# Evacuating the w_up banks by one ScalarE copy, and spreading the first Strassen group over four blocks of the MLP

## The chip, the cores and the metric

The kernel runs on one core of a Trainium2 chip. The metric is the time of one execution on the device, in microseconds.

## The reference

Two layers are computed on 256 tokens of width 1024. Each layer has a pooling mixer, a gated convolution and differential attention, whose branches are gated and merged, then the MLP and a gated embedding. The change touches the MLP alone:

```python
m = rms_norm(h, norm_mlp_g[i])
h = h + jnp.square(jax.nn.relu(m @ w_up[i])) @ w_down[i]
```

`w_up` is 1024 x 4096 and `w_down` 4096 x 1024, all in float32.

## The kernel before

Every weight comes from HBM in units of 128 x 1024 numbers. A unit is split by `WeightStream.prefetch` into a high part `whi` (ACT casts it to float32r, L243) and a low part `wlo` (DVE subtracts, L244). PE then multiplies high by high, high by low and low by high. Splits stand four units ahead of the product that uses them (`AHEAD = 4`), in five pairs of buffers, so a cast for a unit waits until PE has used the buffer's last unit. Transfers of two units each go out on SP's queue into three stage buffers.

The MLP is cut into eight blocks j of 512 hidden columns. A block has four *ups* (m = 0 to 3: 128 hidden columns by 256 tokens, `unit_c`, L414 and L416, one weight unit each) and two *downs* (f = 0, 1; `unit_a`, L376, two weight units each). An up fills a PSUM bank of the pool `bp` (four banks) with two halves of 256 columns, which have to be added, put through ReLU and squared, and split into a high and a low part: `relu_sq_c` (L959 to L965). The first block's ups take another path (`first_up`, `relu_sq`).

For blocks 0, 1 and for blocks 4, 5 (`GROUPS`), the down projection is not done by `unit_a` but by a Strassen scheme of seven products (`("S", j, n)`, `unit_s`, L385 to L389, two weight units each). Products 1, 5, 6 and 7 use `bp` banks: product 5 a bank of its own ("five"), products 1, 6 and 7 share one bank ("chain") that stays taken from product 1 to product 7. Products 2, 3 and 4 add to the downs' `acc` banks. Products 3, 5, 6 and 7 need operands that DVE and ACT make out of the squares of both blocks (`operands`, four steps behind the last up of the second block). Their weights are sums of quarters of `w_down`, made in two buffers of the pool `t8`: one DVE addition (L225) and three accumulating DMAs from POOL's queue (L216).

`mlp_order` lists ups, downs and products; the weights are packed, loaded, split and used in that order. Below it the Tile scheduler orders the instructions of each engine; each engine runs its own list in order. The work outside the MLP has the same order on every engine before and after.

Of the kernel before, what the change touches and what calls it, by code (L numbers as in the profile page):

```python
# [8 lines left out]
F32 = mybir.dt.float32  # L9
F32R = mybir.dt.float32r  # L10
AF = mybir.ActivationFunctionType
ALU = mybir.AluOpType
# [3 lines left out]
S = 256  # L16
# [18 lines left out]
GROUPS = (0, 4)  # L35


def mlp_order():

    order = []  # L40
    for j in range(0, 8, 4):
        order += [("up", b, m) for b in (j, j + 1) for m in range(4)]
        ups = [[("up", b, m), ("up", b, m + 1)] for b in (j + 2, j + 3) for m in (0, 2)]
        downs = [[("down", b, f)] for b in (j + 2, j + 3) for f in range(2)]
        prods = [[("S", j, n) for n in ns] for ns in ((1,), (5,), (3,), (6,), (7, 2), (4,))]
        for n, step in enumerate(ups + downs):
            order += step
            order += prods[n] if n < len(prods) else []
    return order


# [14 lines left out]
def weight_plan():  # L66

    plan = []
    for i in range(DEPTH):
        def a(name, ks, c):
            plan.extend(("A", name, i, k, c) for k in ks)

        def b(name, ks, cs):
            plan.extend(("B", name, i, k, c) for c in cs for k in ks)

        full, half, low, high = (0, 2, 4, 6), (0, 2), (0, 2), (4, 6)
        for ks in (low, high):
            a("w_in", ks, Q)
            a("w_in", ks, K)
        b("w_in", (0, 4), (A_IN, A_IN + 256))
        a("w_in", full, V)
        plan.append(("P", "", i, 0, 0))  # L90
        for c in (C_X, C_C, C_B):
            b("w_in", (0, 4), (c, c + 256))
        for f in range(2):
            a("w_in", full, GATE + f * 512)
        for f in range(2):
            a("w_pool_out", half, f * 512)
        for br, nm in ((1, "w_conv_out"), (2, "w_attn_out")):
            for f in range(2):
                a("w_in", full, GATE + br * D + f * 512)
                a(nm, half, f * 512)  # L100
        for ks in (low, high):
            for f in range(2):
                a("w_o", ks, f * 512)
        a("w_ple_proj", (0,), 0)
        for k in (0, 4):
            b("w_up", (k,), (0, 256))
        for what, j, n in mlp_order():
            if what == "up" and j:
                plan.append(("C", "w_up", i, 0, j * 512 + n * P))
            elif what == "down":  # L110
                a("w_down", (4 * j, 4 * j + 2), n * 512)
            elif what == "S":
                plan.extend(("S", n, i, k, j) for k in (0, 2))
        a("w_ple_proj", (0,), 512)
        for f in range(2):
            a("w_ple_gate", full, f * 512)
    return plan


def quarter(i, j, h, f):  # L120

    return tuple(("A", "w_down", i, 4 * (j + h) + k, 512 * f) for k in (0, 2))


def transfer_plan():


    out = []
    plan = weight_plan()
    u = 0  # L130
    while u < len(plan):
        if plan[u][0] != "S":
            n = 2 if u + 1 < len(plan) and plan[u + 1][0] != "S" else 1
            out.append((tuple(range(u, u + n)), tuple(plan[u:u + n])))
        else:
            n = 2
            _, prod, i, _, j = plan[u]
            at = {1: (0, 0), 3: (1, 1), 2: (1, 0)}.get(prod)
            out.append(((u, u + 1), at and quarter(i, j, *at)))
        u += n  # L140
    return out


def weight_blocks():

    place = {}
    for _, block in transfer_plan():
        if block:
            place.setdefault(block, len(place))
    for i in range(DEPTH):  # L150
        for j in GROUPS:
            place.setdefault(quarter(i, j, 0, 1), len(place))
    return place


class WeightStream:
# [10 lines left out]
    def __init__(self, ctx, tc, w):  # L167
        self.nc = tc.nc
        self.w = w
        self.plan = weight_plan()  # L170
        self.transfers = transfer_plan()
        self.place = weight_blocks()
        self.last_unit = {units[-1]: n for n, (units, _) in enumerate(self.transfers)}
        self.stage_pool = ctx.enter_context(tc.tile_pool(name="wstage", bufs=self.STAGE_BUFS))
        self.part_pool = ctx.enter_context(tc.tile_pool(name="wpart", bufs=self.AHEAD + 1))
        self.keep_pool = ctx.enter_context(tc.tile_pool(name="wkeep", bufs=1))
        self.new_sums = None
        self.sums = {}
        self.stage = {}
        self.parts = {}  # L180
        self.next_dma = 0
        self.next_split = 0
        self.pos = 0

    def load(self, parts=1, between=None):


        while self.next_dma < len(self.transfers):
            units, block = self.transfers[self.next_dma]
            self.next_dma += 1  # L190
            kind, prod, i, _, j = self.plan[units[0]]
            size = len(units) * UNIT
            if kind == "S" and prod == 1:
                if i not in self.sums:
                    self.sums[i] = self.new_sums()
                t, second = self.sums[i]
            elif block:
                t = self.stage_pool.tile([P, 2 * UNIT], F32, tag="stage", name="stage")
            else:
                t = self.sums[i][prod == 7]  # L200
            for n, u in enumerate(units):
                self.stage[u] = t[:, n * UNIT:(n + 1) * UNIT]
            if not block:
                continue
            src = self.w[self.place[block]]
            n = size // parts
            for c in range(0, size, n):
                self.nc.sync.dma_start(out=t[:, c:c + n], in_=src[:, c:c + n])
                if between is not None and c == n:
                    between()  # L210
            if kind == "S" and prod == 1:
                self.nc.sync.dma_start(out=second, in_=self.w[self.place[quarter(i, j, 0, 1)]])
            return
# [4 lines left out]
    def sums_after(self, u):  # L218

        kind, prod, i, k, j = self.plan[u]  # L220
        if kind != "S" or k != 2:
            return
        fst, snd = self.sums[i]
        if prod == 1:
            self.nc.vector.tensor_add(out=fst, in0=fst, in1=snd)  # L225
            self.add_to(snd, i, j, 1, 1)
        elif prod == 5:
            self.add_to(fst, i, j, 1, 1)
        elif prod == 6:
            self.add_to(fst, i, j, 1, 0)  # L230

    def prefetch(self, upto, between=None):
        while self.next_split < min(len(self.plan), upto):
# [28 lines left out]
def kernel(  # L262
# [10 lines left out]
    nc = tc.nc  # L273
# [28 lines left out]
    def t4v(dt=F32):  # L302
        return t4(dt)[:, 0:4 * S].rearrange("p (g t) -> p g t", t=S)

    def t2(dt=F32):
        return u2.tile([P, 512], dt, tag="t2", name="t2")
# [150 lines left out]
    def split(hi, lo, src):  # L457
        nc.scalar.copy(out=hi, in_=src)  # L458
        nc.vector.tensor_sub(out=lo, in0=src, in1=hi.bitcast(F32))  # L459
# [16 lines left out]
    for i in range(DEPTH):  # L476
        units = []
# [458 lines left out]
        def square(j, ms):  # L936

            if j - j % 2 not in GROUPS:
                return t2()[:, 0:S * (ms.stop - ms.start)].rearrange("p (m t) -> p m t", t=S)
            if ms.start == 0:  # L940
                st["f", j] = t4v()
            return st["f", j][:, ms, :]
# [13 lines left out]
        def relu_sq_c(j, m):  # L956
            if m == 0:
                st["s", j] = (t4v(F32R), t4v(F32R))
            sh, sl = st["s", j]  # L959
            bank = tiles.pop(("bp", "up", j, m))  # L960
            z, s2 = t2()[:, 0:S], square(j, slice(m, m + 1))[:, 0, :]
            nc.scalar.copy(out=z, in_=bank[:, 1, :])
            nc.vector.tensor_add(out=z, in0=bank[:, 0, :], in1=z)  # L963
            nc.vector.scalar_tensor_tensor(out=s2, in0=z, scalar=0.0, in1=z, op0=ALU.max, op1=ALU.mult)  # L964
            split(sh[:, m, :], sl[:, m, :], s2)  # L965

        def first_up(m, k):
            xs = st["x"][k // 4].rearrange("p (k a) t -> p k a t", a=2)
# [245 lines left out]
```

## Time and profile before

| | us |
|---|---|
| three runs | 872.79, 873.38, 873.44 |
| median | 873.38 |
| profiled execution, its own time | 872.22 |
| its span, first to last instruction | 870.5 |
| PE busy | 846.5 (97%) |
| DVE busy | 651.5 (75%) |
| ACT busy | 491.9 (57%) |
| a weight sum's transfer on SP's queue, issue to landing, median of 8 | 5.9 |
| one on POOL's queue, median of 12 | 8.8 |

PE is the engine that sets the end: it is busy nearly always, and its few idle stretches lie almost all in the MLP. A busy PE is read with care, since matmuls are pipelined and their ends are modelled; how far apart they start says more. The granted clock was 0.996 of full speed on the mean.

### The profile page before, as it was taken

To read this page: it belongs to the slowest core of one execution; us is meant where nothing else is said; L and a number is where in the kernel's file an instruction comes from. 1 tells how busy PE (TensorE), PEld (TensorE's weight loads), DVE (VectorE), ACT (ScalarE), POOL (GpSimd) and SP (SyncE) were. 2 spreads that over 40 slices of the span, in tenths; PEclk is the share of its full clock that TensorE was granted. 3 is DMA by queue.
4 is the path that set the end of the run, shared out by engine and by line. 5 is a ranking of instruction groups with operands and counts; after the bars stand their busy time and mean duration, and the time that the engine had idled before them with its cause. 6 is when DMAs were issued, how large, how long until landed. Compare 5 with 4: busy or idle time off the path is not lost.

```text
span 870.5 us, 11751 instructions
## 1 busy us (share of the span) xinstructions
PE 846.5 (97%) x4516; PEld 727.9 (84%) x4516; DVE 651.5 (75%) x980; ACT 491.9 (57%) x735; POOL 41.2 (5%) x46
## 2 busy tenths in 40 slices
PE   8999999999997999899999999999999899998997
PEld 6999988888986888788889998888889778887886
DVE  5987886556698858987668887855667978598874
ACT  6655464454666545665654746544456565456562
POOL 2400000000000000000023000000000000000000
PEclk9999999999999999999999999999999999999999
DMA  9755435555657774865445544555556767557541
GB/s 319 280 194 177 163 130 209 194 193 192 244 170 225 248 251 145 236 213 204 174 166 192 194 145 145 182 206 193 194 175 248 209 196 267 216 170 206 180 165 48
DMA packets 25975, 171.02 MB, mean 196 GB/s; under 512 B 3008, under 2 KB 3776, under 8 KB 5952
## 3 DMA queue, kind: packets, MB, share of 16 engines
q1 hardware_dynamic: 24048, 157.66, 49.8%
q0 software_dynamic: 1728, 12.58, 7.6%
q8 instruction: 35, 0.57, 0.3%
q14 instruction: 20, 0.16, 0.1%
q10 hardware_dynamic: 144, 0.05, 0.0%
HBM read 169.23 MB, written 1.05 MB: 196 GB/s over the span
## 4 chain that ended last, share of the span: by engine, by line
PE 92%; DVE 4%; ACT 2%; issue 1%; DMA 1%; SPq 0%; ACTq 0%
PE acc L376 49%; PE bp L414 11%; PE bp L416 5%; PE bp L403 4%; PE bp L405 4%; PE bp L401 4%; DVE wlo L244 2%; PE bp L385 2%; PE bp L387 1%; PE bp L389 1%; PE tr L437 1%; ACT whi L243 1%; PE acc L1128 1%; PE acc L387 1%; PE acc L389 1%
## 5 line engine op out<-in xcount | busy, mean ns | idle before, releaser
L244 DVE TENSOR_TENSOR wlo<-stage,whi 128x1024 fp32r<-128x1024 f32 (+1 forms) x280 | 339.1, 1214 | 168.4 <-ACT whi L243 166.6
L243 ACT CAST whi<-stage 128x1024 fp32r<-128x1024 f32 (+1 forms) x280 | 291.5, 1045 | 273.2 <-PE acc L376 147.7
L376 PE MATMUL acc<-whi,t 128*128 128x512 f32 x1248 | 396.7, 393 | 0.9 <-ACT whi L243 0.6
L376 PEld LDWEIGHTS acc<-whi,t 128*128 128x128 f32 x1248 | 233.7, 188 | 49.4 <-ACT whi L243 1.6
L376 PE MATMUL acc<-wlo,t 128*128 128x512 f32 x624 | 243.6, 390 | 0.5 <-DVE wlo L244 0.5
L376 PEld LDWEIGHTS acc<-wlo,t 128*128 128x128 f32 x624 | 117.2, 188 | 24.9 <-DVE wlo L244 1.6
L414 PE MATMUL bp<-t,whi 128*128 128x512 f32 x448 | 122.4, 395 | 5.4 <-DVE t L963 5.4
L414 PEld LDWEIGHTS bp<-t,whi 128*128 128x128 f32 x448 | 77.3, 189 | 17.7 <-issue 6.6
L401 PE MATMUL bp<-t,whi 128*128 128x256 f32 x320 | 90.5, 284 | 0.0
L403 PE MATMUL bp<-t,whi 128*128 128x256 f32 x320 | 90.5, 283 | 0.0
L405 PE MATMUL bp<-t,wlo 128*128 128x256 f32 x320 | 90.5, 283 | 0.0
L416 PEld LDWEIGHTS bp<-t,wlo 128*128 128x128 f32 x448 | 68.5, 189 | 9.3
L416 PE MATMUL bp<-t,wlo 128*128 128x256 f32 x448 | 71.2, 281 | 0.0
L403 PEld LDWEIGHTS bp<-t,whi 128*128 128x128 f32 x320 | 61.1, 191 | 0.5
L401 PEld LDWEIGHTS bp<-t,whi 128*128 128x128 f32 x320 | 61.0, 191 | 0.5
L405 PEld LDWEIGHTS bp<-t,wlo 128*128 128x128 f32 x320 | 61.1, 191 | 0.1
L244 DVE TENSOR_TENSOR wlo<-t,whi 128x1024 fp32r<-128x1024 f32 x40 | 48.9, 1222 | 11.0 <-ACT whi L243 11.0
L243 ACT CAST whi<-t 128x1024 fp32r<-128x1024 f32 x40 | 42.1, 1051 | 25.8 <-PE bp L414 15.9
L458 ACT CAST t<-t 128x256 fp32r<-128x256 f32 (+1 forms) x80 | 37.4, 469 | 24.5 <-DVE t L964 22.8
L459 DVE TENSOR_TENSOR t<-t,t 128x256 fp32r<-128x256 f32 (+1 forms) x80 | 39.6, 497 | 3.1 <-ACT t L458 2.8
L385 PE MATMUL bp<-whi,t 128*128 128x512 f32 x64 | 26.9, 420 | 11.8 <-DVE t L963 9.6
L427 ACT ACTIVATE t<-tr,par 128x256 fp32r<-128x256 f32 (+1 forms) x56 | 26.2, 502 | 20.9 <-PE tr L568 8.4
(153 smaller groups left out, 778.3 us busy)
## 6 DMA issues: line engine op xcount, KB each, us to landing
stage<-in_w_dram SPq DMA_DIRECT2D x136, 1024.0 KB, 4.8
t<-in_w_dram POOLq DMA_DIRECT2D x12, 1024.0 KB, 8.8
t<-in_w_dram SPq DMA_DIRECT2D x8, 1024.0 KB, 5.9
stage<-in_w_dram SPq DMA_DIRECT2D x4, 512.0 KB, 6.6
stage<-in_w_dram SPq DMA_DIRECT2D x4, 256.0 KB, 5.3
h<-in_x_dram SPq DMA_DIRECT2D x4, 256.0 KB, 10.0
t<-in_xT_dram SPq DMA_DIRECT2D x1, 512.0 KB, 10.1
out_dram<-h SPq DMA_DIRECT2D x2, 256.0 KB, 2.0
```

What stands on the lines that cost most here:

```text
L243: self.nc.scalar.copy(out=hi[:, cs], in_=src[:, cs])
L244: self.nc.vector.tensor_sub(out=lo[:, cs], in0=src[:, cs], in1=hi[:, cs].bitcast(F32))
L376: nc.tensor.matmul(accs[t], lhsT=lhs[:, kx + j, tk], rhs=rhs[:, j, :], start=begins[t] and j == 0 and n == 0, stop=last and j == 1 and n == 2,
L385: nc.tensor.matmul(bank, lhsT=xh[:, k + n, :], rhs=wh[:, n, :], start=first, stop=False, skip_group_check=True)
L401: nc.tensor.matmul(bp[:, m, :], lhsT=wh[:, j, ms], rhs=xh[:, kx + j, :], start=first, stop=False, skip_group_check=True)
L403: nc.tensor.matmul(bp[:, m, :], lhsT=wh[:, j, ms], rhs=xl[:, kx + j, :], start=False, stop=False, skip_group_check=True)
L405: nc.tensor.matmul(bp[:, m, :], lhsT=wl[:, j, ms], rhs=xh[:, kx + j, :], start=False, stop=last, skip_group_check=True)
L414: nc.tensor.matmul(bank, lhsT=wh[:, k, :], rhs=xk[k], start=k == 0, stop=False, skip_group_check=True)
L416: nc.tensor.matmul(bank[:, 1, :], lhsT=wl[:, k, :], rhs=xk[k][:, 0, :], start=False, stop=k == KD - 1, skip_group_check=True)
L427: nc.scalar.activation(out=hi, in_=src, func=AF.Copy, scale=g)
L458: nc.scalar.copy(out=hi, in_=src)
L459: nc.vector.tensor_sub(out=lo, in0=src, in1=hi.bitcast(F32))
```

## The change

Two things change. First, `relu_sq_c`: ACT copies the whole bank (512 columns) into SBUF, DVE adds the two halves there, ACT does the ReLU and squares twice (once into the float32r high part, once into float32), and DVE subtracts for the low part. Before, ACT copied one half, DVE added it to the other half in PSUM, DVE did ReLU and square in one instruction, ACT cast and DVE subtracted. Second, `mlp_order`: the seven products of blocks 0 and 1 no longer stand among the ups and downs of blocks 2 and 3 alone, but are spread up to the ups of block 5. The products of blocks 4 and 5 stand where they stood, up to the downs' end. As the two weight sum buffers are now in use for longer, `load` holds back the first transfer of the second group until product 4 of the first has been split.

```diff
 def mlp_order():
...
+    order = up(0, 0) + up(0, 1) + up(1, 0) + up(1, 1)
+    order += up(2, 0) + prod(0, 1) + up(2, 1) + up(3, 0) + prod(0, 5) + down(2, 0) + up(3, 1) + prod(0, 3)
+    order += down(2, 1) + prod(0, 6) + down(3, 0) + up(4, 0) + prod(0, 7) + down(3, 1) + prod(0, 2)
+    order += up(4, 1) + up(5, 0) + prod(0, 4) + up(5, 1)
+    order += up(6, 0) + prod(4, 1) + up(6, 1) + prod(4, 5) + up(7, 0) + prod(4, 3) + up(7, 1) + prod(4, 6)
+    order += down(6, 0) + prod(4, 7, 2) + down(6, 1) + prod(4, 4) + down(7, 0) + down(7, 1)
     return order
...
+            kind, prod, i, _, j = self.plan[units[0]]
+            if kind == "S" and prod == 1:
+                if self.sums_busy:
+                    self.late += 1
+                    return
+                self.sums_busy = True
             self.next_dma += 1
-            kind, prod, i, _, j = self.plan[units[0]]
...
+        elif prod == 4:
+            self.sums_busy = False
+            late, self.late = self.late, 0
+            for _ in range(late):
+                self.load()
...
-            z, s2 = t2()[:, 0:S], square(j, slice(m, m + 1))[:, 0, :]
-            nc.scalar.copy(out=z, in_=bank[:, 1, :])
-            nc.vector.tensor_add(out=z, in0=bank[:, 0, :], in1=z)
-            nc.vector.scalar_tensor_tensor(out=s2, in0=z, scalar=0.0, in1=z, op0=ALU.max, op1=ALU.mult)
-            split(sh[:, m, :], sl[:, m, :], s2)
+            both = t2().rearrange("p (a t) -> p a t", t=S)
+            nc.scalar.copy(out=both, in_=bank)
+            r = both[:, 0, :]
+            nc.vector.tensor_add(out=r, in0=r, in1=both[:, 1, :])
+            nc.scalar.activation(out=r, in_=r, func=AF.Relu)
+            s2 = both[:, 1, :] if j - j % 2 not in GROUPS else square(j, slice(m, m + 1))[:, 0, :]
+            nc.scalar.activation(out=sh[:, m, :], in_=r, func=AF.Square)
+            nc.scalar.activation(out=s2, in_=r, func=AF.Square)
+            nc.vector.tensor_sub(out=sl[:, m, :], in0=s2, in1=sh[:, m, :].bitcast(F32))
```

The PE list in the first layer, before, behind product 1 of the first group: the second up of that stretch (bank 2573, block 2, m = 3), then product 5 (bank 2603).

```order
L414 MATMUL bp_2573<-t8_2093,whi_2475 128x512 x4
L416 MATMUL bp_2573<-t8_2093,wlo_2476 128x256 x4
L414 MATMUL bp_2573<-t8_2154,whi_2475 128x512 x4
L416 MATMUL bp_2573<-t8_2154,wlo_2476 128x256 x4
L385 MATMUL bp_2603<-whi_2511,t2_2461 128x512
L387 MATMUL bp_2603<-wlo_2512,t2_2461 128x512
L389 MATMUL bp_2603<-whi_2511,t2_2462 128x512
```

The same place after (all line numbers are 18 higher): the same up is bank 2578, then come an up of block 3 (bank 2607) and the first half of down 0 of block 2 (banks acc_2692 and acc_2693).

```order
L432 MATMUL bp_2578<-t8_2093,whi_2479 128x512 x4
L434 MATMUL bp_2578<-t8_2093,wlo_2480 128x256 x4
L432 MATMUL bp_2578<-t8_2154,whi_2479 128x512 x4
L434 MATMUL bp_2578<-t8_2154,wlo_2480 128x256 x4
L432 MATMUL bp_2607<-t8_2093,whi_2515 128x512 x4
L434 MATMUL bp_2607<-t8_2093,wlo_2516 128x256 x4
L432 MATMUL bp_2607<-t8_2154,whi_2515 128x512 x4
L434 MATMUL bp_2607<-t8_2154,wlo_2516 128x256 x4
L394 MATMUL acc_2692<-whi_2608,t4_2469 128x512
L394 MATMUL acc_2693<-whi_2608,t4_2469 128x512
```

Product 5 has moved behind one up more, half a down and a further up. In the second group PE's list is the one of before, but that product 6 stands behind all four ups of block 7.

ACT's list in the second group of the first layer, before: from the cast for product 3's first unit (whi_3395) to the cast for the last up of block 7 (whi_3450). Banks 3265, 3336 and 3364 are ups of block 6 (m = 1, 2, 3); t2_3295 and t2_3358 are the squares of the ups m = 1 and m = 2.

```order
L243 CAST whi_3395<-stage_3205 128x1024
L962 COPY t2_3294<-bp_3265 128x256
L458 CAST t4_3256<-t2_3295 128x256
L458 CAST t2_3314<-t2_3312 128x512
L243 CAST whi_3405<-stage_3205 128x1024
L458 CAST t2_3331<-t2_3329 128x512
L962 COPY t2_3357<-bp_3336 128x256
L243 CAST whi_3420<-stage_3270 128x1024
L962 COPY t2_3387<-bp_3364 128x256
L458 CAST t4_3256<-t2_3358 128x256
L243 CAST whi_3450<-stage_3270 128x1024
```

The same place after: whi_3407 is product 3's first unit, whi_3462 the last up's; bank 3348 is the up m = 2 of block 6, 3376 is m = 3; bank 3406 is product 5; t2_3306 holds the up m = 1, whose bank was copied four rows ahead of this piece.

```order
L261 CAST whi_3407<-stage_3216 128x1024
L476 CAST t2_3326<-t2_3324 128x512
L983 ACTIVATE t2_3306<-t2_3306 128x256
L261 CAST whi_3417<-stage_3216 128x1024
L985 ACTIVATE t4_3268<-t2_3306 128x256
L986 ACTIVATE t2_3306<-t2_3306 128x256
L261 CAST whi_3432<-stage_3282 128x1024
L476 CAST t2_3343<-t2_3341 128x512
L261 CAST whi_3462<-stage_3282 128x1024
L980 COPY t2_3369<-bp_3348 128x512
L980 COPY t2_3399<-bp_3376 128x512
L1056 COPY t2_3429<-bp_3406 128x512
```

The copy of the up m = 1 moved ahead of product 3's cast; the copies of m = 2 and m = 3 moved behind the cast for the last up of block 7. Both layers have the same lists in their MLPs.

## Rows read from the trace of the kernel before

**Rows 1.** The page: busy time, share of the span, instructions of each engine.

```profile
PE 846.5 (97%) x4516; PEld 727.9 (84%) x4516; DVE 651.5 (75%) x980; ACT 491.9 (57%) x735; POOL 41.2 (5%) x46
```

**Rows 2.** Waits of PE: who waited for whom, us in total, times, longest us.

```profile
PE bp L385 <- DVE t L963: 9.6, 4, 2.4
PE bp L414 <- DVE t L963: 5.4, 6, 1.3
PE bp L385 <- ACT whi L243: 2.3, 2, 1.1
```

**Rows 3.** Timeline of PE, first layer: start us, us, instruction, [idle before <-releaser].

```profile
243.23 0.63 PE L416 MATMUL bp<-t,wlo 128*128 128x256 f32 x4
243.70 0.63 PE L414 MATMUL bp<-t,whi 128*128 128x512 f32 x2
...
261.97 0.47 PE L414 MATMUL bp<-t,whi 128*128 128x512 f32 x1 [1.33 <-DVE t L963]
...
267.39 0.47 PE L385 MATMUL bp<-whi,t 128*128 128x512 f32 x1 [2.39 <-DVE t L963]
...
359.03 0.47 PE L385 MATMUL bp<-whi,t 128*128 128x512 f32 x1 [2.39 <-DVE t L963]
```

**Rows 4.** Timeline of DVE and ACT ahead of the wait that ends at 359.03.

```profile
357.20 0.37 ACT L962 COPY t<-bp 128x256 f32<-128x256 f32 x1
357.32 1.23 DVE L244 TENSOR_TENSOR wlo<-stage,whi 128x1024 fp32r<-128x1024 f32 x1 [0.42 <-ACT whi L243]
358.46 0.42 DVE L963 TENSOR_TENSOR t<-bp,t 128x256 f32<-128x256 f32 x1
```

**Rows 5.** Windows: stretch, its us, busy us of each engine, PEclk, DMA share, GB/s.

```profile
318.70:346.80 28.10, 28.10 (x162) 24.55 (x161) 21.93 (x34) 15.04 (x26) 0.88 (x1) 1.00 0.48 157
346.80:378.60 31.80, 28.29 (x147) 23.86 (x146) 28.69 (x46) 21.81 (x35) 1.95 (x4) 1.00 0.85 234
695.10:699.50 4.40, 4.40 (x13) 3.46 (x13) 3.69 (x6) 2.07 (x3) 0.00 (x0) 0.61 0.50 210
267.30:271.70 4.40, 4.31 (x19) 3.63 (x20) 3.95 (x7) 3.35 (x5) 0.00 (x0) 1.00 0.55 222
```

**Rows 6.** Timeline of PE behind the wait that ends at 695.08, second layer.

```profile
695.39 0.39 PE L387 MATMUL bp<-wlo,t 128*128 128x512 f32 x1
695.62 0.39 PE L389 MATMUL bp<-whi,t 128*128 128x512 f32 x1
...
696.54 0.63 PE L389 MATMUL bp<-whi,t 128*128 128x512 f32 x1
696.97 0.63 PE L385 MATMUL bp<-whi,t 128*128 128x512 f32 x1
```

**Rows 7.** Groups by shape, ACT and DVE: xcount | busy us, mean ns | idle.

```profile
L243 ACT CAST whi<-stage 128x1024 fp32r<-128x1024 f32 x276 | 289.1, 1051 | 271.1 <-PE acc L376 147.7 <-PE bp L403 50.7 <-PE bp L414 22.9
...
L458 ACT CAST t<-t 128x256 fp32r<-128x256 f32 x56 | 22.7, 405 | 22.8 <-DVE t L964 22.8
L962 ACT COPY t<-bp 128x256 f32<-128x256 f32 x56 | 20.4, 364 | 0.0
...
L1034 ACT COPY t<-bp 128x512 f32<-128x512 f32 x4 | 2.3, 579 | 0.0
...
L540 ACT ACTIVATE t<-t 128x256 f32<-128x256 f32 x2 | 0.9, 437 | 0.0
...
L244 DVE TENSOR_TENSOR wlo<-stage,whi 128x1024 fp32r<-128x1024 f32 x276 | 336.3, 1221 | 166.3 <-ACT whi L243 164.4
...
L964 DVE SCALAR_TENSOR_TENSOR t<-t 128x256 f32<-128x256 f32 x56 | 23.5, 419 | 0.5
L963 DVE TENSOR_TENSOR t<-bp,t 128x256 f32<-128x256 f32 x56 | 23.3, 417 | 0.0
```

**Rows 8.** Timeline of ACT with a full queue.

```profile
238.42 0.63 ACT L952 ACTIVATE t<-t 128x512 fp32r<-128x512 f32 x1
238.95 0.62 ACT L953 ACTIVATE t<-t 128x512 f32<-128x512 f32 x1
```

More of the change, by code (lines that the diff above doesn't have):

```diff
@@ L38, in mlp_order, with up, down, prod @@
 def mlp_order():
[L40 to L48, printed above, removed]
+    def up(b, half):
+        return [("up", b, m) for m in (2 * half, 2 * half + 1)]
+    def down(b, f):
+        return [("down", b, f)]
+    def prod(j, *ns):
+        return [("S", j, n) for n in ns]
+    order = up(0, 0) + up(0, 1) + up(1, 0) + up(1, 1)
[4 more added lines that the diff above has]
+    order += down(6, 0) + prod(4, 7, 2) + down(6, 1) + prod(4, 4) + down(7, 0) + down(7, 1)
     return order
@@ L178, in __init__ @@
         self.sums = {}
+        self.sums_busy = False
+        self.late = 0
         self.stage = {}
@@ L230, in sums_after @@
             self.add_to(fst, i, j, 1, 0)
+        elif prod == 4:
+            self.sums_busy = False
+            late, self.late = self.late, 0
+            for _ in range(late):
+                self.load()
     def prefetch(self, upto, between=None):
```

## The prediction

> **What bounds the kernel now.** I read the page first: PE is busy 97% of the span [rows 1], and the change neither adds nor removes a matmul. So the most that any change of this kind can give is PE's lost time. The list of PE's waits says where that is: twelve waits, six in each layer, all in the MLP, 9.6 + 5.4 + 2.3 = 17.3 us [rows 2]. Ten of them end on L963, the DVE addition that is the last reader of an up's bank: PE has the weights but no free `bp` bank. The timeline shows two of the largest as a pair in the first layer's first group (1.33 and 2.39 us, ending at 261.97 and 267.39) and the largest of its second group (2.39 us, ending at 359.03) [rows 3].
>
> The idle figure is a little short. A burst of four 256-column matmuls is drawn 0.63 us long although the next burst starts 0.47 us after it [rows 3], so each wait hides 0.16 us more: 12 x 0.16 = 1.9 us, 19.2 us in all.
>
> There is a second cost. After the wait that ends at 695.08 the stretch of 4.40 us has a granted clock of 0.61 of full speed, while behind the equally long wait that ends at 267.39 it stays at 1.00 [rows 5]. At the lower level (1.2 instead of 2.4 GHz) 512-column matmuls start 0.43 us apart instead of 0.23 us [rows 6]; eight of them lose 1.6 us. The mean clock of 0.996 over 870.5 us is 3.5 us of full speed missing, of which a part lies at the very end; I take two such stretches in the second layer, 3.1 us. The removable total is 19.2 + 3.1 = 22.3 us.
>
> Why is L963 late? Ahead of 359.03, ACT's half copy of that bank ends at 357.57, but DVE is in a 1.23 us split until 358.55 and adds only then [rows 4]. In the 31.80 us of the second group's products DVE is busy 28.69 us and ACT 21.81 us [rows 5]. DVE is the full queue, and the bank waits in it.
>
> **Part 1: the bank leaves by ACT.** The bank becomes free with ACT's copy; the addition, then in SBUF, no longer holds it. Per up, ACT gives up the half copy (0.364) and the cast (0.405) and gets a 512-column copy of PSUM (0.579, L1034), a ReLU and two squares [rows 7]. A 256-column ReLU or Square from SBUF isn't in the trace. The nearest rows are the ACTIVATE of L540 (0.437) and the cast of L458 (0.405); with a full queue, instructions start about 0.1 us earlier than their length says (0.63 long, 0.53 apart) [rows 8], which gives 0.34 from below. I take 0.437 of busy time and 0.34 of pace. Busy, an up costs ACT 0.579 + 3 x 0.437 − 0.364 − 0.405 = 1.12 us more; 56 ups make 63 us, 492 to 555 us of the span. DVE loses L964 (0.419): 23.5 us less. The addition of two SBUF operands isn't shown either; its neighbours cost 0.417 and 0.419 whether they read PSUM or not [rows 7], so I leave it at 0.42.
>
> That is 63 us of new work on an engine whose time isn't on the path, so what matters is the pace where ups stand alone. There PE takes 28.10 us for ten ups (162 matmuls recorded, 16 each), 2.81 us each [rows 5]. ACT now needs, at pace, 0.95 (weight cast) + 0.48 + 3 x 0.34 = 2.45 us; with no overlap at all, 1.05 + 0.58 + 1.31 = 2.94 us. I take 2.45, as the order puts the next bank's copy or the next weight cast between an up's dependent steps. So ACT keeps pace with 0.3 us to spare, and costs nothing there; with three or four banks a lag of several us would still be hidden. If that cover were gone at 2.94, the 56 ups would lose 0.13 us each, 7 us.
>
> The Trainium skill speaks against this move: in "ScalarE: Activation LUTs", section "Rules for kernel authors", ReLU, additions and multiplications belong on VectorE and not on ScalarE. The trace has the VectorE as the fuller queue where it counts, so I don't follow it in the forecast; what it would mean is the last rival.
>
> **Part 2: the first group is spread.** I walked the new lists with these durations, with 0 at product 1 of block 0. PE does product 1 to 2.75 (twelve matmuls 0.23 us apart [rows 6]), three ups to 11.2, half a down to 13.9, an up to 16.7, and then asks for product 5's bank. That bank is the one of the second of these ups, filled at 8.4 and copied by ACT at about 14.0. The tightest point is the up in front of product 5: its bank is copied at about 13.0, PE asks at 13.9. Squares for the half down are there with about 1 us to spare too. Then downs (two weight units in 5.5 us instead of in 2.8) thin out the work for ACT and DVE, and nothing is late. So this group's four waits in each layer go, and the slow clock behind one of them.
>
> The held-back load: product 4's split stands some two ups ahead of its use, and four more ups follow it, so that it ends some 2 x 2.8 + 2.75 + 4 x 2.8 = 19.5 us before PE reaches the second group's product 1; such a transfer lands 5.9 us after its issue (the table's median). Hidden, at nothing; wholly exposed it would be 5.9 us per layer.
>
> **Part 3: the second group.** Here the products stand as before. Set 0 at its product 1. PE would do product 1 to 2.75, two ups to 8.35, product 5 to 11.1, product 3 to 13.85 and then the first up of block 7, which takes the bank of block 6's third up. The copies that free the second up's and product 5's banks, walked in the same way, end at 2.1 and 5.4 against 5.55 and 8.35, so both old waits go. But the copy for the up at 13.85 has moved behind the cast for block 7's last up. From 8.1, when PE lets go of the buffer for product 3's first cast, ACT has a full queue: cast to 9.05, operand cast to 9.6, ReLU to 9.9, cast to 10.9, two squares (the first behind the ReLU) to 11.65, cast to 12.6, operand cast to 13.1, cast to 14.05, copy to 14.6. PE waits about 0.7 us for it. That is the new wait, once in each layer: 2 x 0.7 = 1.4 us.
>
> **Sum.** 22.3 − 1.4 = 20.9 us. The profiled execution (872.22, span 870.5) becomes 851.3. The median of the runs is 1.16 us above the profiled time, so the median becomes 852.5.
>
> **Rivals.**
> - *ACT falls behind in the second group.* Without overlap, the eleven instructions of the walk take 0.1 us more each: the wait is 1.8 us instead of 0.7, 2.2 us in all, 854.7; with a slow clock after it in both layers (1.6 each) 857.9. For it: that piece of ACT's list has no gap. Against: the rows with full queues do overlap.
> - *DVE stays late.* The wait moves from the bank to what DVE still makes: the low part of the squares that the half down behind the first group's third up reads, or the low weights. If the first pair's 1.33 + 2.39 + 0.32 = 4.04 us stays in each layer, 8.1 us come back: 860.6. For it: DVE is the fuller queue. Against: it loses 0.42 us per up.
> - *Nothing is gained.* The banks are freed earlier but PE's wait was for the weight splits standing behind the same additions: 873. Against: only two of twelve waits name a weight cast.
> - *ACT sets the pace: slower.* If the five steps of an up run strictly one after the other, with ACT standing still for DVE's addition, an up costs 1.05 + 0.58 + 0.42 + 1.31 = 3.36 us against 2.81. 56 x 0.55 = 31 us are lost against 20.9 gained: 883. It decides from 2.81 + 20.9 / 56 = 3.18 us per up. For it: each ReLU waits for DVE in the middle of ACT's list. Against: other banks' copies and weight casts stand in between. This is where the skill's rule just named would lead; the trace bears it out only so far that ACT gets 63 us more.
>
> **How the numbers follow.** Forecast as summed 0.58 (its own range 850.6 to 853.9: from all 22.3 us and half a microsecond more to twice the new wait); ACT falling behind 0.22; DVE late 0.12; nothing gained 0.03; slower 0.05. The first two hold 0.80, so the range goes from 850.4 to 858.3. A difference under 0.2% (1.7 us) is not told from none by these runs. Faster 0.92, same 0.03, slower 0.05.
>
> **What would show it.** PE's waits on the addition vanish from the list of waits; in their place stands one wait per layer of 0.5 to 1 us on ACT's bank copy, at block 7's first up. The mean clock rises towards 1.00, with no slow stretch after 695 or its like. ACT is busy near 555 us, DVE near 628. Wrong would be: idle time of PE on whole weight casts in the runs of ups (ACT's pace), waits on the low parts in the first group (DVE), or a wait of 2 us and a clock of 1.2 GHz behind the copy.

## The result and the profile after

| | us |
|---|---|
| changed kernel, four runs | 850.20, 850.23, 850.36, 850.93 |
| median | 850.3 |
| kernel before, same session, median of four | 873.41 |
| ratio | 0.9732, 95% interval 0.9714 to 0.975 |
| profiled execution, its span | 850.93, 849.1 |

The kernel became 23.1 us faster. The forecast was 852.5 with a range from 850.4: the direction and the places were right, and the median lies 0.1 us below the range. On the profiled execution, against which the sum was made, 851.3 was forecast and 850.93 came out. Executed again in another session (e13 below), the changed kernel had a median of 851.4.

The page after, busy times of the engines, answers to [rows 1]. PE has 5.4 us less to show as busy although its 4516 matmuls are the same, DVE 19.2 us less, ACT 43.9 us more. PE was idle for 24.0 us of the span before, 17.3 of them in the MLP; it is idle for 8.0 us now, nearly all at the kernel's two ends.

```profile
PE 841.1 (99%) x4516; PEld 724.6 (85%) x4516; DVE 632.3 (74%) x924; ACT 535.8 (63%) x847; POOL 41.2 (5%) x46
```

All of PE's waits after, answering to [rows 2]. None of the old lines is left. The first four stand in the first 15 us, at the kernel's start; only the last, twice 0.2 us, is in the MLP.

```profile
PE acc L394 <- ACT whi L261: 1.1, 2, 0.7
PE tr L343 <- POOL ones L339: 1.0, 1, 1.0
PE acc L394 <- ACT t L445: 0.8, 1, 0.8
PE acc L394 <- DVE wlo L262: 0.5, 1, 0.5
PE acc L405 <- DVE wlo L262: 0.4, 2, 0.2
```

What is left in the second group, first layer: PE at the start of product 1, inside product 3 and at block 7's first up, then ACT's cast and copies ahead of it (start us, us, instruction, idle before).

```profile
341.06 0.40 PE L403 MATMUL bp<-whi,t 128*128 128x512 f32 x1
...
353.55 0.39 PE L403 MATMUL acc<-whi,t 128*128 128x512 f32 x1
354.11 0.50 PE L405 MATMUL acc<-wlo,t 128*128 128x512 f32 x1 [0.18 <-DVE wlo L262]
354.45 0.39 PE L407 MATMUL acc<-whi,t 128*128 128x512 f32 x1
...
355.15 0.39 PE L407 MATMUL acc<-whi,t 128*128 128x512 f32 x1
355.63 1.20 PE L432 MATMUL bp<-t,whi 128*128 128x512 f32 x4
```
```profile
354.05 1.05 ACT L261 CAST whi<-stage 128x1024 fp32r<-128x1024 f32 x1
355.00 1.06 ACT L980 COPY t<-bp 128x512 f32<-128x512 f32 x2
```

These matmuls otherwise start 0.23 us apart. From 353.55 to 354.11 it is 0.56, 0.33 too much, and 0.11 more to the next; from 355.15 to 355.63 it is 0.48, 0.25 too much, and 0.11 more behind that. So each layer keeps 0.8 us, in two pieces: one for product 3's second low part, one for the bank copy that the prediction named. Together with the waits the slow clock went. The stretch that had 0.61 is at 1.00, like the second group's (answering to [rows 5]):

```profile
695.10:699.50 4.40, 4.40 (x25) 3.78 (x24) 2.20 (x4) 2.94 (x6) 0.00 (x0) 1.00 0.72 263
346.80:378.60 31.80, 31.53 (x156) 26.07 (x156) 27.61 (x38) 26.95 (x47) 1.88 (x4) 1.00 0.77 227
```

### The profile page after: what moved, and what is told of

Its sections match the earlier page's. It is cut to its first block, busy times and chain, and to the rows that moved or that the text cites. A ratio compares the mean times of both kernels' runs of the same rounds, so it can differ in the third digit from the quotient of the medians.

```text
span 849.1 us, 11777 instructions
## 1 busy us (share of the span) xinstructions
PE 841.1 (99%) x4516; PEld 724.6 (85%) x4516; DVE 632.3 (74%) x924; ACT 535.8 (63%) x847; POOL 41.2 (5%) x46
## 4 chain that ended last, share of the span: by engine, by line
PE 96%; ACT 1%; DMA 1%; issue 0%; SPq 0%; DVE 0%
PE acc L394 50%; PE bp L432 12%; PE bp L434 6%; PE bp L423 5%; PE bp L421 5%; PE bp L419 5%; PE bp L405 2%; PE bp L407 2%; PE bp L403 2%; PE tr L455 1%; PE acc L1150 1%; PE acc L405 1%; PE acc L407 1%; PE acc L403 1%; DMA stage<-in_w_dram 1%; ACT whi L261 1%
## 5 line engine op out<-in xcount | busy, mean ns | idle before, releaser
L229 POOL DMA_DIRECT2D t<-in_w_dram x12 | 10.7, 888 | 489.5 <-ACT t L986 380.1
L446 DVE SCALAR_TENSOR_TENSOR t<-tr,par,t 128x256 fp32r<-128x256 f32 (+1 forms) x56 | 27.9, 517 | 5.3 <-ACT t L445 5.1
L980 ACT COPY t<-bp 128x512 f32<-128x512 f32 x56 | 31.6, 576 | 0.0
```

What stands on the lines that cost most here:

```text
L446: nc.vector.scalar_tensor_tensor(out=lo, in0=src, scalar=g, in1=hi.bitcast(F32), op0=ALU.mult, op1=ALU.subtract)
L980: nc.scalar.copy(out=both, in_=bank)
```

## Experiments

Line numbers in the versions with the new order are those of the changed kernel. Adding, removing or moving instructions makes the scheduler lay every list anew, so a version can differ from the changed kernel in more than its edit.

**e1: the kernel before, again.** No edit.

> The kernel before, unchanged, to see its own scatter from run to run. Theory (clock): a run's time follows the number of stretches at 1.2 GHz behind the long waits; one stretch takes 3.4 us, lowers the mean granted clock by 0.002 and costs 1.6 us, so runs with a clock of 0.996 take about 872.2 us and those with 0.994 about 873.8 us, and the median lies above the profiled 872.2 because most runs have three or four such stretches where the profile had two. Rival (start): the runs differ by the first 20 us, where PE waits for the first transfers; then the clock is the same in all runs and the times differ by under 1 us. Rival (scale): the profiled time is simply shorter than the others by about 1 us in every kernel.

Median 873.6, ratio 0.9999 (0.9987 to 1.0011). By mean granted clock, the 29 executions of this kernel in that session fall into steps: one at 0.998 (871.12), twelve at 0.996 (871.39 to 872.95), thirteen at 0.994 (873.41 to 874.40), three at 0.992 (875.28 to 875.64). The profiled one had 0.994 and three slow stretches, each around the end of one of the four longest waits (columns as in [rows 5]):

```profile
267.19:270.60 3.41, 3.23 (x8) 2.58 (x9) 2.69 (x6) 1.26 (x3) 0.00 (x0) 0.50 0.70 286
697.27:700.68 3.41, 3.41 (x10) 2.66 (x9) 2.42 (x5) 1.78 (x3) 0.00 (x0) 0.50 0.51 214
789.43:792.84 3.41, 2.97 (x7) 2.42 (x8) 2.95 (x6) 1.03 (x2) 0.00 (x0) 0.50 0.72 300
```

3.41 us at half speed lose 1.7 us, 0.002 of the span: one stretch per step. The execution shown ahead of the prediction had 0.996 and stayed at 1.00 behind 267.39, where this one falls to 0.50. Its two stretches are the one in [rows 5] and this one:

```profile
788.30:791.70 3.40, 3.37 (x8) 2.72 (x9) 2.57 (x5) 1.41 (x3) 0.00 (x0) 0.51 0.61 253
```

So its 872.22 is an execution with two stretches, and the median one has three.

**e2: the new evacuation with the old order.**

```diff
-    order = up(0, 0) + up(0, 1) + ...            # and the held-back load
+    order = []                                   # mlp_order of before
+    for j in range(0, 8, 4): ...
```

> The new evacuation in the old order. Theory (the bank waits in DVE's queue): with the bank freed by ACT both groups are like the second group of the changed kernel, where 0.8 us per layer is left; two groups in two layers leave about 3.2 of 22.3 us, some 854 us, and no stretch at 1.2 GHz. Rival (the order does it): the first group keeps its waits of 5.9 us per layer, some 862 us.

852.23, ratio 0.9757 (0.9738 to 0.9775): the theory, 1.8 us below its figure. Part 1 alone is nearly the whole gain; the first group then has the same leftover as the second, 0.8 us in each layer (the row is the counterpart of the one at 354.11), and these 1.6 us are what the spread is worth. The medians differ by 1.9 us, or by 0.8 if the changed kernel's second median is taken (e13).

```profile
267.98 0.50 PE L387 MATMUL acc<-wlo,t 128*128 128x512 f32 x1 [0.18 <-DVE wlo L244]
```

**e3: the new order with the old evacuation.**

```diff
-            both = ...; nc.scalar.copy(out=both, in_=bank); ...
+            z = t2()[:, 0:S]
+            nc.scalar.copy(out=z, in_=bank[:, 1, :])
+            nc.vector.tensor_add(out=z, in0=bank[:, 0, :], in1=z)
+            nc.vector.scalar_tensor_tensor(out=s2, in0=z, ..., op0=ALU.max, op1=ALU.mult)
+            split(sh[:, m, :], sl[:, m, :], s2)
```

> The new order with the old evacuation. Theory (the bank waits in DVE's queue): the first group's waits go since downs thin out DVE's work, the second group keeps 3.8 us per layer and its stretch at 1.2 GHz in one or both layers: some 860 us. Rival (the order does it): some 853 us. Rival (the order does nothing, the split operands are still late): some 870 us.

867.13, ratio 0.9924 (0.9908 to 0.9941): none of the three figures came. The order is worth 6.3 us, but the first group's waits did not go, even with downs between the ups. The first and the last of PE's four waits in the first layer's first group:

```profile
262.59 1.17 PE L432 MATMUL bp<-t,whi 128*128 128x512 f32 x4 [1.32 <-DVE t L981]
...
274.58 0.70 PE L432 MATMUL bp<-t,whi 128*128 128x512 f32 x2 [1.62 <-DVE t L981]
```

**e4: the bank leaves by ACT, the rest stays.** ReLU and square remain one DVE instruction, with ACT's cast behind it; new order.

```diff
             nc.scalar.copy(out=both, in_=bank)
             nc.vector.tensor_add(out=z, in0=z, in1=both[:, 1, :])
-            nc.scalar.activation(out=r, in_=r, func=AF.Relu)     # and both squares
+            nc.vector.scalar_tensor_tensor(out=s2, in0=z, ..., op0=ALU.max, op1=ALU.mult)
+            split(sh[:, m, :], sl[:, m, :], s2)
```

> The new order; ACT copies the whole bank, but ReLU and square stay one VectorE instruction and ACT casts once, as before. Theory (freeing the bank is what counts): 850 us, the same as the changed kernel within 1 us. Rival (the 0.42 us per up that VectorE is relieved of counts): the second group keeps about half its waits, some 854 us or more.

864.43, ratio 0.9891 (0.9873 to 0.991): the rival's side, but 14.1 us lost instead of some 4. "Free the bank and the wait goes" falls. ACT ahead of PE's longest wait, which ends at 272.81:

```profile
267.48 0.41 ACT L476 CAST t<-t 128x256 fp32r<-128x256 f32 x1 [1.72 <-DVE t L983]
...
268.91 1.06 ACT L261 CAST whi<-stage 128x1024 fp32r<-128x1024 f32 x1 [0.21 <-PE bp L432]
...
271.23 1.04 ACT L261 CAST whi<-stage 128x1024 fp32r<-128x1024 f32 x1 [0.49 <-PE acc L394]
272.18 1.07 ACT L980 COPY t<-bp 128x512 f32<-128x512 f32 x2
```
```profile
272.81 0.96 PE L432 MATMUL bp<-t,whi 128*128 128x512 f32 x3 [1.66 <-ACT t L980]
```

ACT has gaps of 1.72, 0.21 and 0.49 us in front of the copies: they stand behind casts that wait for DVE's squares and for PE's buffers. The bank no longer needs DVE, but its copy's place in the list does.

**e5: the other half: the bank is freed by DVE as before, ReLU and squares on ACT.**

```diff
-            nc.scalar.copy(out=both, in_=bank)
-            nc.vector.tensor_add(out=r, in0=r, in1=both[:, 1, :])
+            nc.scalar.copy(out=r, in_=bank[:, 1, :])
+            nc.vector.tensor_add(out=r, in0=bank[:, 0, :], in1=r)
```

> The changed order, and ReLU and both squares on ACT as in the changed kernel; but the bank leaves as before the change: ACT copies one half of it, and DVE's addition reads the other half from PSUM and frees it. Theory (what counts is that the DVE loses its 0.42 us instruction per up, 23.5 us in all, so that its queue is never behind; who frees the bank is of little weight): about 852, at most 1 us of leftover waits per layer more than the changed kernel. Rival (both halves of the new evacuation are needed, the bank has to leave by ACT too): the waits on the DVE's addition return, 858 to 865, near the 864.4 of the version in which only the copy was changed.

863.71, ratio 0.988 (0.9864 to 0.9897): the rival. DVE ahead of a wait of PE, then that wait: the addition that frees the bank comes behind a low part and an operand's low part.

```profile
270.22 1.23 DVE L262 TENSOR_TENSOR wlo<-stage,whi 128x1024 fp32r<-128x1024 f32 x1 [0.78 <-ACT whi L261]
271.36 0.68 DVE L477 TENSOR_TENSOR t<-t,t 128x512 fp32r<-128x512 f32 x1
271.97 0.42 DVE L981 TENSOR_TENSOR t<-bp,t 128x256 f32<-128x256 f32 x1
```
```profile
272.53 0.47 PE L432 MATMUL bp<-t,whi 128*128 128x512 f32 x1 [1.56 <-DVE t L981]
```

With the new order the four evacuations give 867.1 (old), 864.4 (copy alone), 863.7 (ReLU and squares alone), 850.3 (both): 2.7 and 3.4 us by themselves, 16.8 together.

**e6 and e14: the second group spread like the first.**

```diff
-    order += up(6, 0) + prod(4, 1) + up(6, 1) + prod(4, 5) + up(7, 0) + prod(4, 3) + up(7, 1) + prod(4, 6)
-    order += down(6, 0) + prod(4, 7, 2) + down(6, 1) + prod(4, 4) + down(7, 0) + down(7, 1)
+    order += up(6, 0) + prod(4, 1) + up(6, 1) + up(7, 0) + prod(4, 5) + down(6, 0) + up(7, 1) + prod(4, 3)
+    order += prod(4, 6) + down(6, 1) + prod(4, 7, 2) + prod(4, 4) + down(7, 0) + down(7, 1)
```

> The changed kernel, with the ups and downs of the second group put among its products as in the first one (two ups between product 1 and product 5, a half down behind product 5, product 6 right behind product 3). Theory: the two leftover spots in front of block 7's last ups, 0.8 us in each layer, go, and nothing new comes: 850.3 - 1.6 = 848.7. Rival 1: the leftovers only move to another bank or low part: 850.3. Rival 2: the products stand closer together at the end, their weight sums (8.8 us each from issue to landing) come too late, and PE waits for them: 852 to 858.

848.96, ratio 0.9713 (0.9699 to 0.9728): the theory. Its window in the second group: PE is busy throughout, and its list of waits has no line from the MLP.

```profile
346.80:378.60 31.80, 31.80 (x160) 26.91 (x159) 26.90 (x38) 26.20 (x46) 1.95 (x4) 1.00 0.82 239
```

Beside the changed kernel in one session:

> The version with the second group spread too, beside the changed kernel. Theory (the two leftover spots, 0.8 us in each layer, are gone): 1.3 to 1.6 us below the changed kernel in the same session, about 848.9. Rival (the difference of 1.3 us between the two earlier medians is one of sessions): within 0.5 us of the changed kernel.

849.29 (848.99 to 849.72) against the changed kernel's 851.4. The nine executions of this version in both sessions lie at 849.72 or below, the eight of the changed kernel at 850.13 or above. It is faster than the changed kernel by 1.3 and 2.1 us in the medians of the two sets, once under and once over what was expected. The profiled executions tell the start from the rest: with times counted from the same small matmuls on PE near 25 us, the transposes of L555 (25.37 and 25.22 here, the changed kernel's under e13), they differ by 1.57 us in the first set and by 1.56 in the second. Those are the two spots.

**e13: the changed kernel, again.** No edit.

> The changed kernel once more, unchanged, beside the kernel before in the same session. The prediction added the 1.16 us by which the kernel before's median lay above its profiled execution. Theory (that difference is slow-clock stretches behind PE's waits, whose number differs from run to run; the changed kernel has hardly any wait left): every run at a mean clock of 0.999 or 1.00 and within 1.5 us of each other, median 850.3, 0.3 us either way, at or below its profiled execution. Rival (a profiled execution is about a microsecond shorter than the median whatever the kernel): median 0.8 to 1.4 us above the profiled execution.

851.4 (851.91, 850.13, 851.32, 851.47), ratio 0.9748 (0.9733 to 0.9763), clocks 0.997 to 1.0. The rival is refuted, as the profiled execution, 851.91, is the longest. The theory is met only in part: the runs spread over 1.8 us instead of 1.5, one clock is 0.997, and the median is 0.8 us above the upper end of what was expected. For the profiled execution the profile puts all of it at the start: the MLP has the same two waits of 0.2 us as in the changed kernel's first profile, but the same transposes stand 0.97 us later, and the two times differ by 0.98 us (first profile, then this one):

```profile
25.51 0.60 PE L555 MATMUL tr<-diag,ones 128*128 128x128 f32 x4
```
```profile
26.48 0.60 PE L555 MATMUL tr<-diag,ones 128*128 128x128 f32 x4
```

PE's listed waits at the start are not longer in sum (3.1 us against 3.4), but one of them is 1.59 us long, for a weight cast that itself waited 1.89 us for its transfer, and behind it the clock falls (the last section has the row: 0.70 over 5 us, which is 1.5 us lost).

```profile
10.85 0.73 PE L394 MATMUL acc<-whi,t 128*128 128x512 f32 x2 [1.59 <-ACT whi L261]
```

Two of the other executions took 851.32 and 851.47 at a clock of 1.0; why these were longer than the first session's is open.

**e7 and e8: one and two more Squares per up on ACT.**

```diff
             nc.scalar.activation(out=s2, in_=r, func=AF.Square)
+            nc.scalar.activation(out=s2, in_=r, func=AF.Square)   # e8: twice
```

> The changed kernel with one more 256-column Square per up on ACT, 56 in all, whose result nobody needs (it writes the same values to the same place). Theory (ACT has 0.3 us to spare per up): at 0.34 us of pace each it comes to 2.79 us per up against PE's 2.81, so it costs 0 to 2 us: 850 to 852.5. Rival (ACT already sets the pace where ups stand alone): all 56 x 0.34 = 19 us show: about 869.

> The changed kernel with two more 256-column Squares per up on ACT, 112 in all. Theory (0.3 us to spare per up): the pace is 3.13 us per up against PE's 2.81, so up to 56 x 0.32 = 18 us, less where downs and products let ACT catch up: 856 to 868. Rival 1 (ACT has far more to spare than the sum said, since its share fell short of the predicted 555 us by 19 us): below 853. Rival 2 (ACT already sets the pace): 2 x 19 = 38 us: about 888.

861.96 (ratio 0.9865, 0.9844 to 0.9885) and 865.48 (0.9895, 0.9876 to 0.9914). One more costs 11.7 us, far more than forecast, the second only 3.5. e8 lies in its theory's range, but no account by pace gives both: in e8 PE never waits in the ups that stand alone, and in e7 ACT has idle time ahead of the late copy:

```profile
263.71 1.05 ACT L261 CAST whi<-stage 128x1024 fp32r<-128x1024 f32 x1 [1.76 <-PE bp L432]
...
265.50 0.56 ACT L980 COPY t<-bp 128x512 f32<-128x512 f32 x1
```
```profile
266.12 0.50 PE L432 MATMUL bp<-t,whi 128*128 128x512 f32 x1 [1.97 <-ACT t L980]
```

The copy stands behind a weight cast that waits 1.76 us for a buffer that PE still uses.

**e9 and e10: the added Squares by place.** e9 has two more in the ups of blocks 1, 4 and 5, e10 one more in those of blocks 2, 3, 6 and 7.

```diff
             nc.scalar.activation(out=s2, in_=r, func=AF.Square)
+            if j in (1, 4, 5):                                    # e10: not in, and once
+                nc.scalar.activation(out=s2, in_=r, func=AF.Square)
+                nc.scalar.activation(out=s2, in_=r, func=AF.Square)
```

> The changed kernel with two more 256-column Squares on ACT (their result is needed by nobody) in the ups of blocks 1, 4 and 5 alone, 12 ups in a layer, most of which stand outside the products. The run with one more Square in every up lost 11.6 us, at four spots per layer, all among the products. Theory A (outside the products ACT has room; the loss comes where a bank's copy stands in ACT's list behind a cast that waits): at most 1.5 us lost, 850 to 852. Theory B (ACT is simply too full: what it falls behind in the plain ups, 3.13 - 2.81 = 0.32 us in each of ten, shows as a wait at the first product after them): 2 to 3.2 us per layer, 854 to 857.

> The complement: one more Square in the ups of blocks 2, 3, 6 and 7 alone, 16 in a layer. Theory A (the loss is made among the products): most of the 11.6 us, 858 to 863. Theory B (ACT's sum of work over the whole MLP): about half, and the list among the products bears it: 850 to 855.

864.21 (ratio 0.9898, 0.9877 to 0.9919) and 851.67 (0.9753, 0.9735 to 0.9771): theory A falls in both, the wrong way round. Theory B has e10 in its range, and in e9 the place of the waits, but not their size: the first layer's three come to 5.2 us. (Half of e9's ups, those of block 4 and the first two of block 5, stand among the first group's products, so it keeps the two places less apart than its text says.) ACT at the first of them, with PE's wait behind it, then the same place in e10:

```profile
257.91 1.06 ACT L261 CAST whi<-t 128x1024 fp32r<-128x1024 f32 x1
260.22 1.05 ACT L261 CAST whi<-t 128x1024 fp32r<-128x1024 f32 x1 [1.25 <-PE bp L432]
...
261.69 0.58 ACT L980 COPY t<-bp 128x512 f32<-128x512 f32 x1
```
```profile
262.32 0.50 PE L432 MATMUL bp<-t,whi 128*128 128x512 f32 x1 [1.67 <-ACT t L980]
```
```profile
256.89 1.05 ACT L261 CAST whi<-stage 128x1024 fp32r<-128x1024 f32 x1 [0.29 <-PE bp L407]
257.85 0.58 ACT L980 COPY t<-bp 128x512 f32<-128x512 f32 x1
258.33 1.05 ACT L261 CAST whi<-t 128x1024 fp32r<-128x1024 f32 x1
...
259.80 0.59 ACT L980 COPY t<-bp 128x512 f32<-128x512 f32 x1
260.58 1.05 ACT L261 CAST whi<-t 128x1024 fp32r<-128x1024 f32 x1 [0.19 <-PE bp L432]
```

In e10, as in the changed kernel, the first copy stands ahead of the two casts of `whi<-t`; in e9 it stands behind them, and ACT idles for 1.25 us before it gets there. So with the Squares added to the ups ahead of the group, the copies stand elsewhere in the group's list, and the loss is made there. e8's first layer has the same three waits as e9's (1.67, 1.15 and 2.40 us), although it has more Squares among the products. Whether ACT's added work ahead of the group would cost as much with the copies where the changed kernel has them is not shown.

**e11 and e12: a sixth pair of weight buffers.** Both have e7's extra Square and `bufs=12` for `t2`.

```diff
-        self.part_pool = ...(name="wpart", bufs=self.AHEAD + 1)
+        self.part_pool = ...(name="wpart", bufs=self.AHEAD + 2)   # e12 alone
```

> A control for the next run: one more Square in every up, with 12 instead of 16 small buffers in the pool t2 (which makes room in SBUF). Both theories: as with 16 buffers, 862, 2 us either way.

> One more Square in every up, 12 buffers in the pool t2, and six instead of five buffers for the split weights (whi, wlo). Theory A (the bank's copy is late since it stands behind a weight cast that waits until PE lets go of a buffer; a sixth buffer lets that cast start a unit, 1.4 to 2.8 us, earlier): the waits on the bank's copy, 9.1 us in the run with five, fall to less than half: 851 to 856. Theory B (ACT has too much work among the products, whatever it waits for): no gain against the control, 860 to 863.

861.09 (ratio 0.9858, 0.9834 to 0.9883) for the control, 860.55 (0.9852, 0.9833 to 0.9871) with six. Both lie where theory B had them. The waits on the copy fell from 8.8 to 5.8 us, not below half, and small new ones took up the rest. At e7's spot the weight cast now waits 0.32 us and PE 1.46 instead of the control's 1.97, but an operand's cast that waits for DVE stands ahead of it:

```profile
262.64 0.62 ACT L476 CAST t<-t 128x512 fp32r<-128x512 f32 x1 [0.81 <-DVE t L1019]
263.57 1.05 ACT L261 CAST whi<-stage 128x1024 fp32r<-128x1024 f32 x1 [0.32 <-PE bp L432]
...
264.85 0.57 ACT L980 COPY t<-bp 128x512 f32<-128x512 f32 x1
```

So one more buffer is no remedy. A list held as in the changed kernel, with the extra Squares in it, was not tried; without it, that ACT simply has too much work ahead of or among the products is not excluded, though e10's 32 Squares cost 1.4 us at most.

## Why the prediction was right, and where it failed

*What bounds: right; the removable total: a little small.* 20.9 us were forecast for the profiled execution and 21.3 came, or 21.6 counted from the transposes near 25 us (25.16 before, 25.51 after). The twelve waits went, and the two slow stretches of the second layer with them. With the 1.6 us that are left, 23.2 us were removable instead of 22.3: each slow stretch lost 1.7 us (e1), two 3.4 instead of 3.1, and the other 0.6 is not traced.

*The step that failed* is the last one of the sum: "The median of the runs is 1.16 us above the profiled time, so the median becomes 852.5." It treats the difference as an offset of the measurement. e1 shows that it is one more slow stretch: the profiled execution had two, the median one three. The change removes the waits in front of all of them, so against the median one stretch more was removable than against the profile, and nothing was to be carried over. With that alone the forecast is 851.3, inside its own range; the four runs then lay 0.6 us lower in the median than the profiled one. e13 shows that this much is scatter: its median is 851.4, and the start alone moves by about a microsecond from profile to profile.

*Part 1, ACT's term: too large.* 63 us of busy time were forecast, 43.9 came. The new instructions measured less than taken (answering to [rows 7]):

```profile
L980 ACT COPY t<-bp 128x512 f32<-128x512 f32 x56 | 31.6, 576 | 0.0
L985 ACT ACTIVATE t<-t 128x256 fp32r<-128x256 f32 x56 | 23.3, 415 | 0.5
L986 ACT ACTIVATE t<-t 128x256 f32<-128x256 f32 x56 | 22.6, 404 | 0.0
L983 ACT ACTIVATE t<-t 128x256 f32<-128x256 f32 x56 | 22.5, 413 | 0.0
```

By durations it is 56 x (0.576 + 0.415 + 0.404 + 0.413 − 0.364 − 0.405) = 58.2 us. The other 14.3 us would be the overlap of neighbours in a full queue [rows 8], if the page counts overlapping stretches once; no row shows that sum. The term changed nothing in the forecast, as it was off the path.

*Part 1, its reason: half right.* "The bank becomes free with ACT's copy" was taken to be what removes the waits. By e4 and e5 it takes both: ACT for the bank, and the squares made without DVE, since in e4 ACT's copies stand behind casts, one of which waits 1.72 us for DVE's square. The Trainium skill's rule that ReLU and multiplications belong on VectorE ("ScalarE: Activation LUTs", section "Rules for kernel authors") does not hold here: with them on VectorE the same order takes 864.4 us (e4), with them on ScalarE 850.3.

*Part 1, "0.3 us to spare per up": not what decides.* It was said of ups that stand alone, and there PE waits for nothing even in e8, where the sum puts ACT's pace at 3.13 us per up against PE's 2.81. But e7 and e9 lose 11.7 and 13.9 us among the products, with ACT idle in front of the late copies. A margin in pace says nothing of the order in which the next version's list is laid.

*Part 2: the walk was right.* Product 5 was put at 16.7 us behind product 1; it starts at 271.96, product 1 at 255.25: 16.71. The bank copies were put at about 13.0 and 14.0, 268.25 and 269.25 on this scale; ACT does three in a row from 267.67, the last ending at 269.23. The up at 13.9 (269.18) starts without a wait. But the order is not what makes that room: part 1 with the old order has lost only the 0.8 us per layer shown in e2, and the new order alone keeps four waits there (e3).

```profile
255.25 0.40 PE L403 MATMUL bp<-whi,t 128*128 128x512 f32 x1
...
269.18 1.07 PE L432 MATMUL bp<-t,whi 128*128 128x512 f32 x4
...
271.96 0.40 PE L403 MATMUL bp<-whi,t 128*128 128x512 f32 x1
```
```profile
267.67 1.56 ACT L980 COPY t<-bp 128x512 f32<-128x512 f32 x3
```

*Part 3: right in time, with one piece left out.* The walk has PE ask for block 7's first up at 13.85 and get it at 14.6, 354.91 and 355.66 on this scale (product 1 starts at 341.06); the up starts at 355.63. But 0.44 of the 0.8 us lies earlier, at product 3's low part, which the walk left out because it followed ACT alone; it is taken from the wait for the copy, so the total fits although only 0.36 lies at the place named. PE's list of waits names no copy, against the sign that the prediction gave. e6 removes both pieces.

*The rivals.* ACT falling behind in the second group (1.8 us per layer), DVE late (4.04) and nothing gained did not come. The version that kept DVE's square (e4) has a wait at the half down that the second names, 1.0 us in each layer, but for the squares' cast on ACT, which stands behind a weight cast that waits 1.74 us for PE. ACT setting the pace did not come either.

## What to carry to other kernels

Before a profile's time is set against a median, look at the granted clock of each: if waits are followed by slow stretches in some executions, a change that removes the waits also removes the difference. Where engines run their lists in order, ask of a late instruction not how busy its engine is but which waiting instruction stands ahead of it. And where a scheduler lays the lists, an added instruction is no clean probe of load: compare the lists at the place where the time is lost, which may be far from the edit.

## What the runs showed of the hardware that was not expected

The same waits of some 2.4 us were followed by 3.41 us at 1.2 instead of 2.4 GHz in some executions and not in others: two of four places in the profile of before, three of four in e1. At the start of e13 a stretch at the lower level followed a wait of 1.59 us (10 to 15 us has a granted clock of 0.70; PE was busy for 3.76 of the 5 us before that), while e5, with waits of up to 1.6 us in the MLP, has a mean clock of 0.999 to 1.0 in every execution.

```profile
10.00:15.00 5.00, 4.15 (x11) 3.02 (x12) 3.10 (x4) 3.65 (x5) 0.00 (x0) 0.70 1.01 417
```
